# Feed-forward up projections: one 512-column product for the weight's high part, first group partly in the D banks, down projection two groups behind

## The chip, the cores and the metric

One core of a Trainium2 chip. The metric is the device time of one launch in microseconds, as the median of several runs. TensorE multiplies; VectorE, ScalarE and GpSimd (POOL) work on what it needs and leaves; loads from HBM are issued by SP's queue. Each engine works through its own instructions in program order.

## The reference, cut to what matters

A 4-layer encoder over 256 tokens of width 1024. Each layer is a SwiGLU feed-forward (FFN) half-step, a token mixer (attention, convolution, Fourier or gated linear attention) and a second FFN half-step, so there are eight FFN stages:

```python
def _swiglu(h, w1, w3, w2):
    return (jax.nn.silu(h @ w1) * (h @ w3)) @ w2

def reference(x, ...):
    h = x
    for i in range(DEPTH):                       # DEPTH = 4
        h = h + 0.5 * _swiglu(_rmsnorm(h, norm_g[i, 0]), ffn_w1[i, 0], ffn_w3[i, 0], ffn_w2[i, 0])
        u = _rmsnorm(h, norm_g[i, 1])
        ...                                      # mix = one of four mixers of u
        h = h + mix
        h = h + 0.5 * _swiglu(_rmsnorm(h, norm_g[i, 2]), ffn_w1[i, 1], ffn_w3[i, 1], ffn_w2[i, 1])
    return _rmsnorm(h, final_norm_g)
```

## The kernel before, in words

All is kept transposed: features on the 128 partitions, 256 tokens along the free axis. Weights and activations are float32. To multiply them in TensorE's fp32r form without losing bits, every operand is split into a high part (the value rounded to fp32r) and a low part (the rest), and a product is the sum of three: high times high, low of the one times high of the other, and the other way round (`mm3`, with the single product in line 69). The moving operand has 256 columns.

Weights come in blocks of 128x2048 (1 MB), in the order in which `plan` lists them. A load (`dma_block`, line 141, issued by SP) fills one of four `raw` buffers; `split_block` makes the high part `wh` on ScalarE (line 151) and the low part `wl` on VectorE (line 154), or on GpSimd where it is told so, into one of four pairs of buffers, and issues the next load. `done` counts blocks that TensorE has used up, and `pump(n)` splits as many new ones, at the place in the program where it is called.

An FFN stage (`ffn`) has 11 groups (NG) of 256 hidden features. `up(i, ...)` computes one 128x512 product per matrix: 8 steps k over the input features, 2 halves c of 128 hidden features, 3 products each, 48 in all, into one PSUM bank of the tag `ab`, of which there are four, used in turn. In the texts A0 is w1's product of group 0, B0 is w3's, and so on. `evac_a` multiplies A by the row factor R on VectorE (line 441) and applies silu on ScalarE (line 442); `evac_b` multiplies B by R (447), multiplies both (448) and splits the result into `gh` (ScalarE, 517) and `gl` (VectorE, 518). `down_add` adds w2's 48 products of a group into the four banks D0 to D3, which are held through the stage.

R is the normalization factor 1/rms of the tokens, spread over the partitions. x isn't multiplied by it before the up projection; the evacuations are. So `stats(True)` computes R while the first group's products run: two products with ones, then `newton_rsqrt` on VectorE, two integer operations and three steps of three operations (lines 348 to 356). In stages behind the first one it splits two weight blocks between, one of them on GpSimd.

The order of TensorE in a stage: A0 and B0 (k by k in turn, with `stats` behind k = 4, in the first stage behind k = 7), A1, B1, down of group 0, A2, B2, down of group 1, and so on. `DOWN_AFTER` says behind which group which down projection runs; groups 9 and 10 go into `down_final`, which finishes D0 to D3 one after the other, while `close_pair` adds them to h and makes the next stage's x. VectorE's and ScalarE's order is that of the program: at group 1 first the split and the evacuation of A0 and B0, then `evac_a` of A1, then two splits (`pump`), then B1's products and `evac_b(1)`. All is in program order on each engine (a manual schedule).

Of the kernel before, what the change touches and what calls it, by code (L numbers as in the profile page):

```python
# [21 lines left out]
DOWN_AFTER = {i: i - 1 for i in range(1, NG - 2)}  # L22
DOWN_AFTER[NG - 1] = NG - 3
NR = 4
NW = 4
# [15 lines left out]
class Enc:  # L41
# [31 lines left out]

    def mm3(self, out, l, r, start, stop, passes=(0, 1, 2)):
        (lh, ll), (rh, rl) = l, r
        for p in passes:
            self.mm(out, (lh, lh, ll)[p], (rh, rl, rh)[p], start and p == 0, stop and p == 2)
# [65 lines left out]
    def split_block(self, between=None, eng=None):  # L143
        b = self.nsplit
        if b >= len(self.blocks):
            return
        self.nsplit += 1
        raw = self.raw.pop(b)
        wh = self.sb(self.wp, [128, 2048], F32R, "wh", NW)
        wl = self.sb(self.wp, [128, 2048], F32R, "wl", NW)  # L150
        self.nc.scalar.activation(wh, raw, AF.Copy)  # L151
        if between:
            between()
        (eng or self.nc.vector).tensor_tensor(wl, raw, f32(wh), ALU.subtract)  # L154
        self.wsp[b] = (wh, wl)
        self.dma_block()

    def take(self, key):
        b = self.ntake
        self.ntake += 1  # L160
        assert self.blocks[b][0] == key, (self.blocks[b][0], key)
        wh, wl = self.wsp.pop(b)
        r = lambda t: t.rearrange("p (a b) -> p a b", a=self.blocks[b][1])
        return r(wh), r(wl)
# [17 lines left out]
    def setup(self):  # L182
# [9 lines left out]
        for b in first:  # L192
            self.raw[b] = self.sb(self.wp, [128, 2048], F32, "raw", NR)
            self.wsp[b] = (self.sb(self.wp, [128, 2048], F32R, "wh", NW), self.sb(self.wp, [128, 2048], F32R, "wl", NW))
# [19 lines left out]
        for j in range(4):  # L214
            self.normed(j)
            s = slice(512 * j, 512 * j + 512)
            for b in first:
                wh, wl = self.wsp[b]
                self.split(self.raw[b][:, s], wh[:, s], wl[:, s])
# [53 lines left out]
    def normed(self, j, h=None):  # L273
# [3 lines left out]
        if self.nstage < len(self.stages):  # L277
            xh = self.sb(self.hp, [128, 2, 256], F32R, f"xh{j}")
            xl = self.sb(self.hp, [128, 2, 256], F32R, f"xl{j}")
# [5 lines left out]
            self.xn[j] = (xh, xl)  # L285
        else:

            y = f32(self.sb(self.hp, [128, 2, 256], F32R, f"xh{j}"))
# [5 lines left out]
    def square(self, j, h=None, before_split=None):  # L294
# [17 lines left out]
        if j == 3:  # L312
# [5 lines left out]
            if self.row_norm():  # L318
                self.nsq = [self.sb(self.hp, [128, 256], F32R, "R", 2) for _ in range(2)]
                self.split(self.acc[:, 0], *self.nsq)  # L320
# [16 lines left out]
    def xk(self, k, t=None):  # L337
        xh, xl = self.x[k // 2]
        if t is None:
            return xh[:, k % 2, :], xl[:, k % 2, :]  # L340
        return xh[:, k % 2, 128 * t:128 * t + 128], xl[:, k % 2, 128 * t:128 * t + 128]

    def newton_rsqrt(self, y, r, shape, tag, bufs=2, pool=False):
# [6 lines left out]
        if pool:  # L350
            self.pump(1)
            self.pump(1, eng=nc.gpsimd)
        for n in range(3):
            nc.vector.tensor_tensor(t, r, r, ALU.mult)  # L354
            nc.vector.scalar_tensor_tensor(u, t, -0.5, y, ALU.mult, ALU.mult)  # L355
            nc.vector.scalar_tensor_tensor(r, u, 1.5, r, ALU.add, ALU.mult)  # L356

# [23 lines left out]
    def stats(self, row=False, scale=1.0):  # L381

        if row:
# [6 lines left out]
            self.newton_rsqrt(y, self.R, [128, 256], "nR", 1, self.nstage > 0)  # L390
            return
# [25 lines left out]
    def ffn(self, l, s):  # L417
# [6 lines left out]
        def up(i, names, hook={}):  # L424

            ws = [self.take((n, i)) for n in names]
            ps = [self.ab() for _ in names]
            for k in range(8):
                for w, p in zip(ws, ps):
                    for c in range(2):  # L430
                        sl = slice(128 * c, 128 * c + 128)
                        self.mm3(p[:, 256 * c:256 * c + 256], (w[0][:, k, sl], w[1][:, k, sl]), self.xk(k),
                                 start=k == 0 and c == 0, stop=k == 7)
# [5 lines left out]
        def evac_a(A):  # L439
            sl = self.sb(self.ev, [128, 2, 256], F32, "sl", 2)  # L440
            nc.vector.tensor_tensor(sl, self.v2(A), self.Rb(), ALU.mult)  # L441
# [3 lines left out]
        def evac_b(i, sl, B):  # L445
            br = self.sb(self.ev, [128, 2, 256], F32, "br", 2)
            nc.vector.tensor_tensor(br, self.v2(B), self.Rb(), ALU.mult)  # L447
            nc.vector.tensor_tensor(br, sl, br, ALU.mult)  # L448
            gh = self.sb(self.ev, [128, 2, 256], F32R, "gh", 3)
            gl = self.sb(self.ev, [128, 2, 256], F32R, "gl", 3)  # L450
            self.split(br, gh, gl)
            g[i] = (gh, gl)

        self.down_begin()
        first = self.nstage == 0
        A0, B0 = up(0, ("w1", "w3"), {7 if first else 4: lambda: self.stats(True)})
        for i in range(1, NG):
            A, = up(i, ("w1",))
            if i == 1:
                s0 = []  # L460
                self.pump(1, between=lambda: s0.append(evac_a(A0)), eng=nc.gpsimd if first else None)
                evac_b(0, s0[0] if s0 else evac_a(A0), B0)
            sl = evac_a(A)
# [24 lines left out]
    def dmm(self, w, g, d, k, stop=False, passes=(0, 1, 2)):  # L488
        if self.D4 is None:
# [4 lines left out]
                 (w[0][:, k, 128 * d:128 * d + 128], w[1][:, k, 128 * d:128 * d + 128]),  # L494
                 (g[0][:, k], g[1][:, k]), start=self.dfirst[j], stop=stop, passes=passes)
# [20 lines left out]
    def split(self, src, hi, lo):  # L516
        self.nc.scalar.activation(hi, src, AF.Copy)  # L517
        self.nc.vector.tensor_tensor(lo, src, f32(hi), ALU.subtract)  # L518
# [38 lines left out]
    def mix1(self):  # L557
# [13 lines left out]
        def pw1(i, names=("pa", "pg"), hook={}):  # L571
            ws = [self.take((n, i)) for n in names]
            ps = [self.ab() for _ in names]
            for k in range(8):
                for w, p in zip(ws, ps):
                    for c in range(2):
                        sl = slice(128 * c, 128 * c + 128)
                        self.mm3(p[:, 256 * c:256 * c + 256], (w[0][:, k, sl], w[1][:, k, sl]), self.xk(k),
# [95 lines left out]
        A0, G0 = pw1(0, hook={4: lambda: self.stats(True)})  # L674
# [88 lines left out]
        nn = self.sb(ev, [128, 4, 2, 256], F32R, "zs", 3)  # L763
        for i in range(4):
            if i < 2:
                hi, lo = (self.sb(self.hp, [128, 2, 256], F32R, f"x{t}{i}") for t in "hl")
            else:
                hi, lo = nn[:, 2 * i - 4], nn[:, 2 * i - 3]
# [9 lines left out]
            if i:  # L778
                for c in range(2):
                    self.split(zc[i][:, c], hi[:, c], lo[:, c])  # L780
            g.append((hi, lo))
# [21 lines left out]
    def mix2(self):  # L803
# [10 lines left out]
        def s1(g, banks):  # L814
            for t in range(2):
                for kk in range(2):
                    self.mm3(banks[t][:, 0:260], self.xk(2 * g + kk, t), tuple(half(w, kk) for w in cs),
                             start=kk == 0, stop=kk == 1)
            return banks

        def e1(g, banks):
            for t in range(2):
                h = self.sb(self.ev, [128, 260], F32R, f"a{g}{t}h")
                l = self.sb(self.ev, [128, 260], F32R, f"a{g}{t}l")
# [3 lines left out]
                ab[g][t] = (h, l)  # L828

        def s2(j):  # L830
# [3 lines left out]
            for c in range(2):  # L834
                for t in range(2):
                    for q in range(2):
# [3 lines left out]
                        h, l = ab[j][t]  # L840
                        self.mm3(p[:, 256 * c:256 * c + 256], (h[:, o:o + 128], l[:, o:o + 128]),
                                 (cs[0][:, t, r], cs[1][:, t, r]), start=n == 0, stop=t == 1 and q == 1)
                        n += 1
            gh = self.sb(self.ev, [128, 2, 256], F32R, f"m{j}h")
            gl = self.sb(self.ev, [128, 2, 256], F32R, f"m{j}l")
            self.split(self.v2(p), gh, gl)
            return gh, gl
# [29 lines left out]
    def mix0(self):  # L877
# [8 lines left out]
        def vproj(g, hf, hook=None):  # L886
            w = self.take(("v", g, hf))
            p = self.ab()
            for k in range(8):
                for t in range(2):  # L890
                    self.mm3(p[:, 256 * t:256 * t + 256], self.xk(k, t), (w[0][:, k, :], w[1][:, k, :]),
# [25 lines left out]
        def proj(hp, g):  # L917

            def step(k, state={}):
# [4 lines left out]
                for c in range(2):  # L924
                    sl = slice(128 * c, 128 * c + 128)
                    self.mm3(p[:, 256 * c:256 * c + 256], (w[0][:, k, sl], w[1][:, k, sl]), self.xk(k),
# [63 lines left out]
        def V(hp):  # L990
# [12 lines left out]
            if c == 0:  # L1003
                og[j] = (self.sb(ev, [128, 2, 256], F32R, f"og{j}h"), self.sb(ev, [128, 2, 256], F32R, f"og{j}l"))
            self.split(p[:, 0:256], og[j][0][:, c], og[j][1][:, c])
# [41 lines left out]
    def pre3(self):  # L1047
# [11 lines left out]
        wah, wal = self.sb(P, [128, 8, 64], F32R, "wah"), self.sb(P, [128, 8, 64], F32R, "wal")  # L1059
        self.split(wa, wah, wal)  # L1060
# [14 lines left out]
        return wah, wal, wa2, tri, lst, mask  # L1075

    def mix3(self):
# [15 lines left out]
        wah, wal, wa2, tri, lst, mask = self.pre  # L1093
# [6 lines left out]
        def qkproj(i, hook=None):  # L1100
            w = self.take(("gqk", i))
            p = self.ab()
            for k in range(8):
                for c in range(2):
                    sl = slice(128 * c, 128 * c + 128)
                    self.mm3(p[:, 256 * c:256 * c + 256], (w[0][:, k, sl], w[1][:, k, sl]), self.xk(k),
# [18 lines left out]
        for k in range(8):  # L1125
            self.mm3(pa[0:64, 0:256], (wah[:, k], wal[:, k]), self.xk(k), start=k == 0, stop=k == 7)
# [29 lines left out]
        def gate_c(d, t):  # L1156
            h = self.sb(ev, [128, 512], F32R, f"la{d}{t}h")
            l = self.sb(ev, [128, 512], F32R, f"la{d}{t}l")
            self.split(za[d, t], h, l)
            la[d, t] = (h, l)  # L1160
# [10 lines left out]
        def vproj(i):  # L1171

            def step(k, s):
# [3 lines left out]
                for t in range(2):  # L1177
                    self.mm3(p[:, 256 * t:256 * t + 256], self.xk(k, t), (w[0][:, k, :], w[1][:, k, :]),
# [11 lines left out]
        def rproj(i):  # L1190
            def step(k, s):
# [3 lines left out]
                for t in range(2):  # L1195
                    self.mm3(p[:, 256 * t:256 * t + 256], self.xk(k, t), (w[0][:, k, :], w[1][:, k, :]),
# [12 lines left out]
        def kstate():  # L1209

            for t in range(2):
# [5 lines left out]
                for d in range(2):  # L1217
                    p = bank()
                    h, l = la[d, t]
# [7 lines left out]
        og = {}  # L1227

        def head(hd):
# [4 lines left out]
            def decay(d):  # L1234
                p = bank()
                for t in range(2):
                    h, l = la[d, t]
# [45 lines left out]
            def out():  # L1283
# [19 lines left out]
                pool, tg = (self.hp, "x%s%d") if hd >= 2 else (ev, "og%s%d")  # L1303
                gh = self.sb(pool, [128, 2, 256], F32R, tg % ("h", hd))
                gl = self.sb(pool, [128, 2, 256], F32R, tg % ("l", hd))
                og[hd] = (gh, gl, o)

            def trans():
                gh, gl, o = og[hd]
# [221 lines left out]
```

## Time and profile before

| | before |
|---|---|
| median of 3 runs | 2022.13 us (2021.82 to 2023.69) |
| profiled execution | 2023.73 us, its span 2022.0 us |
| TensorE products busy | 1962.7 us, 97% of the span, 16496 products |
| VectorE busy | 1281.7 us, 63% |
| ScalarE busy | 898.5 us, 44% |
| GpSimd busy | 122.6 us, 6% |
| granted TensorE clock, mean | 0.987 of full speed |
| DMA | 338.59 MB, 167 GB/s in the mean |

Products are pipelined: a row's duration (0.28 us for 256 columns) reaches past the start of the next one. What a product costs in a dense stretch is read from the step between two starts, or from a stretch of the chain divided by its count. The time between a wait's end and the modelled end of the product before it is what the profile calls idle. The granted clock has two levels here, full speed (1.0, 2.4 GHz) and half (0.5, 1.2 GHz); a value between is a mean over a stretch.

### The profile page before, as it was taken

What the parts mean: (1) busy time and instruction counts of PE and PEld (TensorE: products, weight loads), DVE (VectorE), ACT (ScalarE), POOL (GpSimd) and SP (SyncE); (2) the same over time, 40 slices, a digit from 0 to 9 for tenths busy, and PEclk for the clock granted to TensorE, in tenths of its full rate; (3) what the DMA queues carried; (4) which work ended last, traced back from release to release, by engine and by line L of the source; (5) the groups of instructions that cost most, each with busy time, mean ns of one, the idle gap of its engine ahead of it and who ended that gap; (6) DMA issues with size and microseconds to landing.
All of it is one profiled execution on the core that took longest, in us unless ns stands there. A gap on an engine that the chain in (4) does not pass through costs nothing.

```text
span 2022.0 us, 36938 instructions
## 1 busy us (share of the span) xinstructions
PE 1962.7 (97%) x16496; PEld 1925.5 (95%) x16496; DVE 1281.7 (63%) x1374; ACT 898.5 (44%) x936; POOL 122.6 (6%) x93
## 2 busy tenths in 40 slices
PE   7999999999999998699999999999999999999998
PEld 7999999999999997499999999999999999999998
DVE  6655567755675575786557655765576555767554
ACT  4433544533444343444334444544444435754433
POOL 2000000000060011410001000000010000001000
PEclk9999999999999999799999999999999999999999
DMA  6555533455455533045554554355545554334551
GB/s 227 214 187 188 188 136 126 167 189 187 146 211 189 187 141 133 4 165 210 185 188 162 194 187 146 127 207 188 188 146 214 188 181 165 126 125 168 189 187 42
DMA packets 48671, 338.59 MB, mean 167 GB/s; under 512 B 5568, under 2 KB 5744, under 8 KB 8192
## 3 DMA queue, kind: packets, MB, share of 16 engines
q1 hardware_dynamic: 47952, 335.11, 45.5%
q8 instruction: 129, 2.11, 0.4%
q0 software_dynamic: 560, 1.12, 0.2%
q14 instruction: 30, 0.25, 0.0%
HBM read 335.16 MB, written 1.05 MB: 166 GB/s over the span
## 4 chain that ended last, share of the span: by engine, by line
PE 86%; DVE 9%; ACT 2%; issue 1%; DMA 0%; SPq 0%; POOL 0%; DVEq 0%; ACTq 0%; POOLq 0%
PE ab L69 55%; PE D L69 31%; DVE wl L154 2%; DVE nRt L354 2%; DVE zc L647 1%; ACT wh L151 1%; DVE nRu L348 0%; DVE R L356 0%; DVE nRu L355 0%; DMA raw<-in_ffn_w_dram 0%; PE D L72 0%; DVE gl L518 0%; DVE br L448 0%; PE ab L72 0%; DVE R L518 0%
## 5 line engine op out<-in xcount | busy, mean ns | idle before, releaser
L154 DVE TENSOR_TENSOR wl<-raw,wh 128x2048 fp32r<-128x2048 f32 x304 | 694.3, 2294 | 414.2 <-ACT wh L151 413.9
L69 PE MATMUL ab<-xh,wh 128*128 128x256 f32 x3200 | 911.3, 285 | 8.6 <-ACT wh L517 7.4
L69 PE MATMUL ab<-xh,wl 128*128 128x256 f32 x3200 | 908.7, 284 | 3.1 <-DVE wl L154 3.1
L69 PE MATMUL ab<-xl,wh 128*128 128x256 f32 x3200 | 908.5, 284 | 0.0
L151 ACT ACTIVATE wh<-raw 128x2048 fp32r<-128x2048 f32 x315 | 595.1, 1904 | 109.1 <-issue 84.0
L69 PEld LDWEIGHTS ab<-xh,wh 128*128 128x128 f32 x3200 | 617.4, 193 | 14.3 <-ACT wh L517 7.4
L69 PEld LDWEIGHTS ab<-xh,wl 128*128 128x128 f32 x3200 | 617.2, 193 | 3.5 <-DVE wl L154 3.3
L69 PEld LDWEIGHTS ab<-xl,wh 128*128 128x128 f32 x3200 | 617.2, 193 | 0.0
L69 PE MATMUL D<-gh,wh 128*128 128x256 f32 x1408 | 396.9, 282 | 7.3 <-ACT gh L517 7.3
L69 PE MATMUL D<-gl,wh 128*128 128x256 f32 x1408 | 400.5, 284 | 2.4 <-DVE gl L518 2.4
L69 PE MATMUL D<-gh,wl 128*128 128x256 f32 x1408 | 398.9, 283 | 0.0
L69 PEld LDWEIGHTS D<-gh,wh 128*128 128x128 f32 x1408 | 268.9, 191 | 8.5 <-ACT gh L517 8.5
L69 PEld LDWEIGHTS D<-gl,wh 128*128 128x128 f32 x1408 | 265.2, 188 | 3.9 <-DVE gl L518 3.9
L69 PEld LDWEIGHTS D<-gh,wl 128*128 128x128 f32 x1408 | 265.8, 189 | 0.0
L442 ACT ACTIVATE sl<-sl 128x512 f32<-128x512 f32 x88 | 55.6, 632 | 348.6 <-DVE sl L441 348.6
L517 ACT ACTIVATE gh<-br 128x512 fp32r<-128x512 f32 x88 | 55.6, 632 | 338.0 <-DVE br L448 338.0
L154 POOL TENSOR_TENSOR wl<-raw,wh 128x2048 fp32r<-128x2048 f32 x11 | 57.6, 5240 | 1135.4 <-ACT wh L151 805.4
L441 DVE TENSOR_TENSOR sl<-ab,R 128x512 f32<-128x512 f32 x88 | 60.6, 689 | 76.5 <-PE ab L69 75.7
L518 DVE TENSOR_TENSOR gl<-br,gh 128x512 fp32r<-128x512 f32 x88 | 61.4, 697 | 61.5 <-ACT gh L517 61.5
L282 ACT ACTIVATE xh<-h,cols 128x256 fp32r<-128x256 f32 x88 | 39.9, 500 | 73.8 <-DVE h L261 61.8
L447 DVE TENSOR_TENSOR br<-ab,R 128x512 f32<-128x512 f32 x88 | 60.6, 689 | 13.4 <-PE ab L69 13.4
L448 DVE TENSOR_TENSOR br<-sl,br 128x512 f32<-128x512 f32 x88 | 61.4, 698 | 4.9 <-ACT sl L442 1.4
(451 smaller groups left out, 1536.1 us busy)
## 6 DMA issues: line engine op xcount, KB each, us to landing
raw<-in_ffn_w_dram SPq DMA_DIRECT2D x262, 1024.0 KB, 4.8
raw<-in_attn_w_qk_dram SPq DMA_DIRECT2D x12, 1024.0 KB, 4.8
raw<-in_conv_w_pw_dram SPq DMA_DIRECT2D x12, 1024.0 KB, 4.8
raw<-in_gla_w_in_dram SPq DMA_DIRECT2D x12, 1024.0 KB, 4.8
raw<-in_attn_w_v_dram SPq DMA_DIRECT2D x6, 1024.0 KB, 4.8
raw<-in_fnet_w_dram SPq DMA_DIRECT2D x4, 1024.0 KB, 4.7
raw<-in_gla_w_o_dram SPq DMA_DIRECT2D x4, 1024.0 KB, 4.8
raw<-in_ffn_w_dram SPq DMA_DIRECT2D x8, 256.0 KB, 6.8
```

Of the source, the lines that this page charges most:

```text
L69: return self.nc.tensor.matmul(out, lhsT, rhs, start=start, stop=stop, skip_group_check=True)
L151: self.nc.scalar.activation(wh, raw, AF.Copy)
L154: (eng or self.nc.vector).tensor_tensor(wl, raw, f32(wh), ALU.subtract)
L282: nc.scalar.activation(xh[:, c], h[:, c], AF.Copy, scale=g[c])
L354: nc.vector.tensor_tensor(t, r, r, ALU.mult)
L441: nc.vector.tensor_tensor(sl, self.v2(A), self.Rb(), ALU.mult)
L442: nc.scalar.activation(sl, sl, AF.Silu)
L447: nc.vector.tensor_tensor(br, self.v2(B), self.Rb(), ALU.mult)
L448: nc.vector.tensor_tensor(br, sl, br, ALU.mult)
L517: self.nc.scalar.activation(hi, src, AF.Copy)
L518: self.nc.vector.tensor_tensor(lo, src, f32(hi), ALU.subtract)
L647: nc.vector.scalar_tensor_tensor(o, x, w, o, ALU.mult, ALU.add)
```

## The change

In `ffn`, and nowhere else in the arithmetic: for each k and half c, w's low part times x's high part is one product of 256 columns, and w's high part times both parts of x, which now lie side by side in one tile, is one of 512 columns. They fill a bank: the left half sums low times high and high times high, the right half high times low. So a product of a group takes two banks, one for each half c, and `both` brings the halves together: a ScalarE copy of the right half and a VectorE add of the left, for each bank. A's two banks come from `ab`, also B's, but for group 0, where B0 takes D1 and D2. R is multiplied behind that, into A's tile ahead of silu, and once more behind silu. The down projection of group i runs behind group i + 2. The Newton steps come back as a list: `factor` runs the short operations and one split behind k = 4; the first step follows A0's `both`, then a split, then the other two steps. No split in the FFN or conv stage's factor runs on GpSimd any more. All other edits rename the two parts of an operand into one tile of pairs; in the conv stage `factor` has two splits about the three steps.

```diff
-DOWN_AFTER = {i: i - 1 for i in range(1, NG - 2)}
-DOWN_AFTER[NG - 1] = NG - 3
+DOWN_AFTER = {i: i - 2 for i in range(2, NG)}
...
+    def pair(self, pool, shape, tag, bufs=1):
+
+        return self.sb(pool, [shape[0], 2, *shape[1:]], F32R, tag, bufs)
+
     def mm3(self, out, l, r, start, stop, passes=(0, 1, 2)):
-        (lh, ll), (rh, rl) = l, r
+
         for p in passes:
-            self.mm(out, (lh, lh, ll)[p], (rh, rl, rh)[p], start and p == 0, stop and p == 2)
+            self.mm(out, l[:, (0, 0, 1)[p]], r[:, (0, 1, 0)[p]], start and p == 0, stop and p == 2)
...
+    def newton_rsqrt(self, y, r, shape, tag, bufs=2, later=0):
 
         nc = self.nc
         t = self.sb(self.ev, shape, F32, tag + "t", bufs)
         u = self.sb(self.ev, shape, F32, tag + "u", bufs)
         nc.vector.tensor_scalar(u.bitcast(I32), y.bitcast(I32), 1, None, ALU.logical_shift_right)
         nc.vector.tensor_scalar(r.bitcast(I32), u.bitcast(I32), -1, 0x5F3759DF, ALU.mult, ALU.add)
-        if pool:
-            self.pump(1)
-            self.pump(1, eng=nc.gpsimd)
-        for n in range(3):
+
+        def step():
             nc.vector.tensor_tensor(t, r, r, ALU.mult)
             nc.vector.scalar_tensor_tensor(u, t, -0.5, y, ALU.mult, ALU.mult)
             nc.vector.scalar_tensor_tensor(r, u, 1.5, r, ALU.add, ALU.mult)
+
+        for _ in range(3 - later):
+            step()
+        return [step] * later
 
...
-            self.newton_rsqrt(y, self.R, [128, 256], "nR", 1, self.nstage > 0)
-            return
+            return self.newton_rsqrt(y, self.R, [128, 256], "nR", 1, 3)
...
         def up(i, names, hook={}):
 
+
             ws = [self.take((n, i)) for n in names]
-            ps = [self.ab() for _ in names]
+            ps = [[self.dbank(c + 1) if n else self.ab() for c in range(2)] for n in range(len(names))]
             for k in range(8):
+                x = self.xk(k)
                 for w, p in zip(ws, ps):
                     for c in range(2):
                         sl = slice(128 * c, 128 * c + 128)
-                        self.mm3(p[:, 256 * c:256 * c + 256], (w[0][:, k, sl], w[1][:, k, sl]), self.xk(k),
-                                 start=k == 0 and c == 0, stop=k == 7)
+                        self.mm(p[c][:, 0:256], w[:, 1, k, sl], x[:, 0], k == 0, False)
+                        self.mm(p[c].rearrange("p (q n) -> p q n", q=2), w[:, 0, k, sl], x, False, k == 7)
                 if k in hook:
                     hook[k]()
             self.done(len(names))
             return ps
 
-        def evac_a(A):
-            sl = self.sb(self.ev, [128, 2, 256], F32, "sl", 2)
-            nc.vector.tensor_tensor(sl, self.v2(A), self.Rb(), ALU.mult)
+        def both(ps, tag):
+
+            t = self.sb(self.ev, [128, 2, 256], F32, tag, 2)
+            for c in range(2):
+                nc.scalar.activation(t[:, c], ps[c][:, 256:512], AF.Copy)
+            for c in range(2):
+                nc.vector.tensor_tensor(t[:, c], t[:, c], ps[c][:, 0:256], ALU.add)
+            return t
+
+        def act_a(sl):
+            nc.vector.tensor_tensor(sl, sl, self.Rb(), ALU.mult)
             nc.scalar.activation(sl, sl, AF.Silu)
             return sl
 
         def evac_b(i, sl, B):
-            br = self.sb(self.ev, [128, 2, 256], F32, "br", 2)
-            nc.vector.tensor_tensor(br, self.v2(B), self.Rb(), ALU.mult)
+            nc.vector.tensor_tensor(sl, sl, self.Rb(), ALU.mult)
+            br = both(B, "br")
             nc.vector.tensor_tensor(br, sl, br, ALU.mult)
-            gh = self.sb(self.ev, [128, 2, 256], F32R, "gh", 3)
-            gl = self.sb(self.ev, [128, 2, 256], F32R, "gl", 3)
-            self.split(br, gh, gl)
-            g[i] = (gh, gl)
+            g[i] = self.pair(self.ev, [128, 2, 256], "g", 3)
+            self.split(br, g[i])
 
         self.down_begin()
-        first = self.nstage == 0
-        A0, B0 = up(0, ("w1", "w3"), {7 if first else 4: lambda: self.stats(True)})
+        steps = []
+
+        def factor():
+            steps.extend(self.stats(True))
+            self.pump(1)
+
+        A0, B0 = up(0, ("w1", "w3"), {4 if self.nstage else 7: factor})
+
+        sl0 = both(A0, "sl")
+        steps.pop(0)()
+        self.pump(1)
+        for f in steps:
+            f()
         for i in range(1, NG):
             A, = up(i, ("w1",))
+            sl = both(A, "sl")
             if i == 1:
-                s0 = []
-                self.pump(1, between=lambda: s0.append(evac_a(A0)), eng=nc.gpsimd if first else None)
-                evac_b(0, s0[0] if s0 else evac_a(A0), B0)
-            sl = evac_a(A)
+                self.pump(1)
+                evac_b(0, act_a(sl0), B0)
+            act_a(sl)
             self.pump()
...
+        def factor():
+            steps = self.stats(True)
+            self.pump(1)
+            for f in steps:
+                f()
+            self.pump(1)
+
+        A0, G0 = pw1(0, hook={4: factor})
         self.pump()
```

## Rows read from the trace of the kernel before

**Rows 1.** The page: busy time of the engines; the chain's shares by engine.

```profile
PE 1962.7 (97%) x16496; PEld 1925.5 (95%) x16496; DVE 1281.7 (63%) x1374; ACT 898.5 (44%) x936; POOL 122.6 (6%) x93
...
PE 86%; DVE 9%; ACT 2%; issue 1%; DMA 0%; SPq 0%; POOL 0%; DVEq 0%; ACTq 0%; POOLq 0%
```

**Rows 2.** The chain in order of time (start us, us, what), one group.

```profile
595.62 11.52 PE ab L69 x96
607.13 5.76 PE D L69 x48
```

**Rows 3.** Timeline of TensorE (start us, us): 512-column products, then 256-column ones.

```profile
1730.45 0.39 PE L69 MATMUL ab<-la00l,lst 128*128 128x512 f32 x1
1730.68 0.40 PE L69 MATMUL D<-la10h,lst 128*128 128x512 f32 x1
1730.92 0.40 PE L69 MATMUL D<-la10l,lst 128*128 128x512 f32 x1
1731.15 0.60 PE L72 MATMUL ab<-ident,kT 128*128 128x128 f32 x4
...
1731.82 0.40 PE L69 MATMUL D<-la01l,lst 128*128 128x512 f32 x1
...
1732.53 0.28 PE L69 MATMUL D<-tri,la00h 128*128 128x256 f32 x1
...
1732.88 0.28 PE L69 MATMUL D<-tri,la01l 128*128 128x256 f32 x1
```

**Rows 4.** Timeline of TensorE where a stage's second group ends; idle time in brackets.

```profile
568.37 0.28 PE L69 MATMUL ab<-xh,wl 128*128 128x256 f32 x1
570.02 0.39 PE L69 MATMUL D<-gh,wh 128*128 128x256 f32 x1 [1.36 <-ACT gh L517]
...
571.28 0.42 PE L69 MATMUL D<-gh,wl 128*128 128x256 f32 x1
...
571.92 0.41 PE L69 MATMUL D<-gh,wl 128*128 128x256 f32 x1
```

**Rows 5.** Who TensorE waited for: us in total, times, longest us.

```profile
PE D L69 <- ACT gh L517: 7.3, 6, 1.8
...
PE ab L69 <- DVE wl L154: 3.1, 1, 3.1
PE D L69 <- DVE gl L518: 2.4, 7, 0.5
```

**Rows 6.** Busy time by stretch, PEclk the mean granted clock; pauses, then a whole group.

```profile
571.40:578.20 6.80, 6.80 (x48) 6.80 (x47) 4.30 (x3) 4.23 (x3) 6.80 (x7) 0.78 0.21 65
...
1315.90:1329.90 14.00, 14.00 (x95) 14.00 (x96) 10.32 (x16) 6.22 (x6) 0.00 (x0) 0.78 0.51 193
595.50:612.80 17.30, 17.30 (x146) 17.30 (x146) 11.51 (x9) 8.78 (x7) 0.00 (x0) 1.00 0.62 237
```

**Rows 7.** Timeline of VectorE in the stage that starts at 545.2.

```profile
552.85 0.42 DVE L389 TENSOR_SCALAR R<-D 128x256 f32<-128x256 f32 x1
...
554.17 2.29 DVE L154 TENSOR_TENSOR wl<-raw,wh 128x2048 fp32r<-128x2048 f32 x1 [0.16 <-ACT wh L151]
556.38 4.85 DVE L354 TENSOR_TENSOR nRt<-R 128x256 f32<-128x256 f32 x1
...
564.48 0.43 DVE L356 SCALAR_TENSOR_TENSOR R<-nRu,R 128x256 f32<-128x256 f32 x1
565.01 0.69 DVE L441 TENSOR_TENSOR sl<-ab,R 128x512 f32<-128x512 f32 x1
...
573.99 5.02 DVE L154 TENSOR_TENSOR wl<-raw,wh 128x2048 fp32r<-128x2048 f32 x2 [2.50 <-ACT wh L151]
578.93 0.68 DVE L447 TENSOR_TENSOR br<-ab,R 128x512 f32<-128x512 f32 x1
```

**Rows 8.** A ScalarE copy out of PSUM: ns min/median/max, first and last start us.

```profile
L408 ACT ACTIVATE R<-D x2: 386/393/400, 226.5 to 1704.9; 128x256 f32<-128x256 f32 x2
```

**Rows 9.** A VectorE operation of 128x256 out of PSUM.

```profile
L389 DVE TENSOR_SCALAR R<-D x9: 418/425/425, 28.5 to 1826.6; 128x256 f32<-128x256 f32 x9
```

**Rows 10.** Timeline of GpSimd in that stage: its split.

```profile
556.02 4.93 POOL L154 TENSOR_TENSOR wl<-raw,wh 128x2048 fp32r<-128x2048 f32 x1 [5.94 <-ACT wh L151]
```

## What I expect, and from which rows

> **What bounds the kernel now.** I read the page first: TensorE carries 86% of the chain that ended last, VectorE 9% [rows 1]. The chain in order of time shows what the TensorE share is made of: inside a feed-forward stage it is an even beat, 96 up products in 11.52 us, then 48 down products in 5.76 us, with nothing between [rows 2]. That is 120.0 ns a product of 256 columns. Eight stages of 11 such groups of 17.28 us are 1,521 of the 2,022 us. In a whole group the other engines have room: VectorE is busy 11.5 of 17.3 us, ScalarE 8.8 [rows 6]. So two things are worth money: the price of a product, and what interrupts the beat. The list of waits names the interruptions in the feed-forward stages: 7.3 us for gh, 2.4 us for gl, 3.1 us for wl [rows 5]. They lie at one place of a stage, behind its first two groups of up products. Take the stage that starts at 545.2 (B1's last product starts at 568.37; it and the 193 before it at 120 ns lead back there): TensorE then stands until 570.02 for gh, and goes on in steps of about 215 ns [rows 4], because the granted clock has fallen (0.78 on average over the next 6.8 us [rows 6]). What it waits for is one line of work on VectorE, in program order: the factor R, the evacuation of A0 and B0, and weight splits of 2.3 us among them [rows 7].
>
> **The change, part by part.**
>
> *The wide product.* In each of 8 x 11 x 2 x 2 x 8 = 2,816 places (stage, group, matrix, half, k) three products of 256 columns become one of 256 and one of 512. Before: 360 ns. The trace has the new form: high and low parts times lst in 512 columns. Three steps of the first run, 1730.45 to 1731.15, take 233 ns each, three of the second, 1731.82 to 1732.53, 237; the 256-column products right behind them step by 117 [rows 3]. So the time goes with the columns; there is hardly a fixed part to save. I take 119 + 235 = 354 ns, 6 ns less, 16.9 us in all. Bounds: 2 x 120 = 240 ns for the wide one in the up products' own beat (no gain), and 106.7 ns of columns at 2.4 GHz plus the 13.3 ns that the 120 holds beside them, so 226.7 ns, 37 us gained. I take the value next to the 235 rows.
>
> The Trainium skill, page "TensorE: Matmul & The Clock Gate", section "Back-to-back issue gap", states a gap of N/2.4 + 2.5 ns, 216 ns at 512 columns. The rows do not agree (235, and 120 at 256). If the wide product reached 216 beside an unchanged 120, the part would be an estimated 68 us; that is a rival below.
>
> *The evacuation.* A product now fills two banks (x high and low side by side in each). It takes two ScalarE copies and two VectorE adds of 128x256 more; nearest rows 0.39 us [rows 8] and 0.43 us [rows 9], 0.44 taken with the issue. Per group VectorE takes on 4 x 0.43 = 1.7 us and ScalarE 1.6: 13.2 and 10.4 of 17 us, under TensorE's beat, which hides it; without that cover it would be 3.3 us a group.
>
> *The banks.* Four ab banks held four products; now they hold two. A0 takes ab 0 and 1, B0 takes D1 and D2, A1 ab 2 and 3, B1 ab 0 and 1, A2 ab 2 and 3, **B2 ab 0 and 1**, so B2 may start only when B1 has been evacuated. In the steady beat B1's successor comes 11 us later: nothing. At the start of a stage it decides, because of the next part. D1 and D2 have been read by the close of the stage before, whose last 2.9 us of products lie behind; nothing taken, 0.5 us a stage if VectorE lags.
>
> *The down projection one group later.* It takes 5.76 us of products out from between B1 and A2. TensorE then runs A0, B0, A1, B1, A2, B2 without a pause and wants w3 of group 2 and B1's banks 5.7 us earlier than the present order would. VectorE's list for it is no shorter. With S the start of the stage: the factor's three short operations and the split of w1 of group 1 end at 11.2, as now (552.85 and 554.17 [rows 7], S = 545.2). Two adds for A0 to 12.6, a Newton step of three operations to 14.0, the split of w3 to 16.3, two steps to 19.0, adds for A1 to 19.9. The split of w1 of group 2 runs 20.3 to 22.6: ScalarE's part stands behind A1's copies (A1 ends at 17.2). Then evac of A0, B0 and act of A1, which ping-pong between the two engines (multiply, silu, multiply, two adds, multiply, gh, gl, multiply, at 0.65 to 0.9 each): 28.3. silu 29.0, ScalarE's half of the split of w3 30.9, then **two** VectorE splits, w3 of group 2 and w2 of group 0, as pump() issues both before evac_b(1): 35.5 (the pair is the 5.02 us row at 573.99, and B1's first operation stands behind it at 578.93 today, too [rows 7]). One multiply and the first add: 36.6. TensorE is through with A2 at 28.7. **So it waits 7.9 us at B2**, with all of its queue behind it (B2, then the first down products). With every gap on VectorE closed the same work (23.6 us from 7.6 on) would end at 31.2: 2.5 us, the floor. In the first stage the factor comes behind its first group, and two splits are already done; the same list gives 5.4 us. Seven times 7.9 and 5.4: 60.7 us.
>
> After such a pause the clock is low for a while: 1.0 us lost over 48 products (6.80 for 5.76) after the shorter pause, 2.6 over 95 (14.0 for 11.4) after the 3.1 us one [rows 6]. I take 1.8 a stage, 14.4 us.
>
> *What goes.* The present waits for gh, gl and wl, 12.8 us, with 0.16 us for each of 14 because the wait is counted from the product's modelled end, 2.2; and their low clock, 2.6 + 1.0 + about 1.0 in the other stage of that form. Together 20 us. The GpSimd split goes with it: while it runs (556.02 to 560.95 [rows 10]) VectorE's first Newton operation takes 4.85 us, where the next of its kind take 0.43 [rows 7]. That is already in the forward list above (R ends at 19.0 instead of 564.91 - 545.2 = 19.7; the split that moves to VectorE eats the gain). On POOL what stands behind that split (the conv stage's preparation) starts earlier, and nobody waits for it. Raw loads on SP are released by the split that reads them, four ahead; the ones that a split now on VectorE releases arrive before they are wanted. Renamed pairs, the order lo before hi, and the conv stage's two splits: nothing, 1 us either way.
>
> Sum: 60.7 + 14.4 - 20 - 16.9 = +38 us. The profiled run took 2023.7 (span 2022.0 and 1.7 around it), 1.6 over the median, so 2,060 as a median.
>
> **Rivals.**
> 1. *The wide product streams at nearly one column a cycle* (512 in 216 ns). Then 24 ns go in each place, 68 us, the pause grows by some 0.7 us a stage, and the sum is about -7 (60.7 + 5.6 + 14.4 - 20 - 68): 2,015 us, faster. For it: the skill's gap rule above. Against it: six steps of 233 to 237 ns in the same data form. It decides the sign from about 20 ns saved a place on.
> 2. *The pause at B2 is near its floor*: ScalarE runs ahead so far that VectorE has no gaps. 8 x 2.5 + 10 of clock - 20 - 16.9 gives -7: 2,015 us, faster. For it: ScalarE has the time. Against it: the trace shows the same ping-pong today (VectorE idles 2.50 us before the pair of splits at 573.99, for ScalarE's part [rows 7]). It turns the sign at a pause of about 3.5 us a stage.
> 3. *The wide product saves nothing* (240 ns, the beat of 120 per 256 columns holds): the change then only pays the pause, 59 + 14.4 - 20: 2,076 us.
>
> **How the numbers follow.** Forecast 2,060, chance 0.62, its own range 2,040 to 2,078 (pause 7 to 9 us, clock 1.0 to 2.6, 2 to 13 ns saved a place). Rival 1: 0.12. Rival 2: 0.14. Rival 3: 0.12. Faster by over 0.2% (4 us, about what a measurement of this kernel can tell from no change): most of rivals 1 and 2, 0.23; within: 0.05; slower: 0.72. The range takes in rivals 1 and 2 about their middle and rival 3: 2,012 to 2,080.
>
> **What will show it.** A wait of TensorE of 7 to 9 us before a w3 product of the third group in each stage, released by VectorE's add, with a low granted clock behind it; steps of 119 and 235 ns in the up products; a steady group of about 17.1 us; no wait at the first down products; VectorE's first Newton operation at 0.43 us. It would be wrong if the steps were 216, or if evac_b(1) ran ahead of its splits.

## The result and the profile after

The changed kernel takes 2042.93 us as the median of 4 runs (2040.49 to 2043.78), the kernel before beside it 2022.47 us (2021.82 to 2023.69, 4 runs). The ratio is 1.0098, with a 95% interval of 1.0081 to 1.0116: 20 us slower. The profiled execution of after took 2040.49 us, its span is 2038.7 us against 2022.0, and the mean granted clock 0.976 against 0.987.

The page of after, its engines (the same view as [rows 1]):

```profile
PE 1939.5 (95%) x13680; PEld 1777.0 (87%) x13680; DVE 1385.3 (68%) x1735; ACT 1016.8 (50%) x1288; POOL 70.7 (3%) x84
```

TensorE has 2,816 products fewer and is busy for 23 us less, yet the span has grown by 17: what it gained, and more, it now spends standing. The list of waits of TensorE says where (the same view as [rows 5]; columns: who waits for whom, us in total, times, the longest):

```profile
PE ab L68 <- DVE br L446: 53.8, 8, 8.9
PE D L68 <- DVE R L320: 4.3, 1, 4.3
PE D L68 <- DVE h L260: 1.4, 1, 1.4
PE ab L68 <- DVE w L156: 1.4, 1, 1.4
```

The waits for gh and gl are gone. In their place stands one wait, once in each of the eight stages, for `br`: the sum of B's two halves. The chain of after in order of time through the stage that starts at 1074.82 shows who is late (start us, us, engine and what):

```profile
1086.32 5.21 PE ab L68 x30
...
1092.29 1.81 ACT w L153
1094.10 0.02 issue
1094.12 2.29 DVE w L156
1096.41 0.61 DVE sl L450
...
1097.05 0.64 ACT sl L451
...
1102.36 1.91 ACT w L153
1104.26 0.02 issue
1104.29 0.04 DVE w L156
1104.32 2.17 issue
1106.49 2.29 DVE w L156
1108.78 0.60 DVE sl L455
1109.38 0.34 DVE br L446
1109.72 0.04 issue
1109.77 7.92 PE ab L68 x32
1117.69 5.76 PE D L68 x48
1123.45 11.10 PE ab L68 x64
```

From 1091 on the chain leaves TensorE and runs through VectorE and ScalarE by turns until B1's first half has been added, 1109.72. Only then may B2 start: it uses the banks in which B1 lies. Two things more stand in the last three lines. B2's 32 products take 7.92 us (0.16 of it the modelled end of the last), where 64 in the next group take 11.10, so 5.55 for 32: the clock is low for them, 0.78 in the mean over the stretch from 1109.77 to 1120 that is shown below. And a group of 64 up products and 48 down products lasts 16.86 us, against 17.28 before [rows 2].

TensorE's own timeline at the stage's start and about the pause (compare [rows 4]), and two windows of after: a steady group, and the stretch behind the pause (compare [rows 6]; columns of the windows: us, busy time of PE, PEld, DVE, ACT and POOL, granted clock, DMA share, GB/s):

```profile
1074.82 0.86 PE L68 MATMUL ab<-x,w 128*128 128x256 f32 x4
...
1101.76 1.20 PE L68 MATMUL ab<-x,w 128*128 128x256 f32 x6
1109.77 2.50 PE L68 MATMUL ab<-x,w 128*128 128x256 f32 x7 [6.81 <-DVE br L446]
```

```profile
600.42:617.28 16.86, 16.86 (x114) 15.46 (x114) 11.49 (x12) 9.82 (x11) 0.00 (x0) 1.00 0.60 225
1109.77:1120.00 10.23, 10.23 (x53) 9.19 (x54) 5.86 (x8) 5.95 (x8) 0.00 (x0) 0.78 0.64 241
```

VectorE's timeline in the same stage (compare [rows 7]):

```profile
1083.19 2.28 DVE L156 TENSOR_TENSOR w<-raw,w 128x2048 fp32r<-128x2048 f32 x1
...
1086.46 0.42 DVE L350 TENSOR_TENSOR nRt<-R 128x256 f32<-128x256 f32 x1
...
1104.29 4.50 DVE L156 TENSOR_TENSOR w<-raw,w 128x2048 fp32r<-128x2048 f32 x2 [2.50 <-ACT w L153]
...
1109.30 0.74 DVE L446 TENSOR_TENSOR br<-br,ab 128x256 f32<-128x256 f32 x2
```

The first Newton operation takes 0.42 us, not 4.85; no GpSimd split runs beside it now. The pair of splits of 4.50 us, with 2.50 us of waiting for ScalarE's part in front of it, stands between A1's evacuation and B1's, as the prediction had placed it.

### The profile page after: what moved, and what is told of

Read it like the earlier page. It is cut to its first block, busy times and chain, and to the rows that moved or that the text cites. A ratio compares the mean times of both kernels' runs of the same rounds, so it can differ in the third digit from the quotient of the medians.

```text
span 2038.7 us, 31966 instructions
## 1 busy us (share of the span) xinstructions
PE 1939.5 (95%) x13680; PEld 1777.0 (87%) x13680; DVE 1385.3 (68%) x1735; ACT 1016.8 (50%) x1288; POOL 70.7 (3%) x84
## 4 chain that ended last, share of the span: by engine, by line
PE 86%; DVE 7%; ACT 4%; issue 2%; DMA 0%; SPq 0%; POOL 0%; DVEq 0%; ACTq 0%; POOLq 0%
PE ab L68 53%; PE D L68 32%; DVE w L156 3%; ACT w L153 2%; DVE zc L664 1%; DVE sl L450 1%; DVE sl L455 1%; DVE br L446 0%; DMA h<-in_x_dram 0%; PE D L71 0%; DVE br L457 0%; ACT sl L444 0%; ACT sl L451 0%; ACT g L534 0%; PE ab L71 0%
## 5 line engine op out<-in xcount | busy, mean ns | idle before, releaser
L68 PE MATMUL ab<-x,w 128*128 128x256 f32 (+1 forms) x6528 | 1124.6, 331 | 63.7 <-DVE br L446 53.8
L68 PEld LDWEIGHTS ab<-x,w 128*128 128x128 f32 x6528 | 980.5, 192 | 187.3 <-DVE br L446 56.4
L156 DVE TENSOR_TENSOR w<-raw,w 128x2048 fp32r<-128x2048 f32 x313 | 714.1, 2293 | 360.3 <-ACT w L153 358.0
L153 ACT ACTIVATE w<-raw 128x2048 fp32r<-128x2048 f32 x315 | 595.7, 1904 | 38.5 <-ACT w L153 21.8
L68 PEld LDWEIGHTS D<-g,w 128*128 128x128 f32 x4224 | 516.2, 188 | 3.0
L68 PE MATMUL D<-g,w 128*128 128x256 f32 x4224 | 518.5, 282 | 0.0
L446 DVE TENSOR_TENSOR sl<-sl,ab 128x256 f32<-128x256 f32 x176 | 66.7, 418 | 61.6 <-ACT sl L444 61.5
L68 PE MATMUL D<-x,w 128*128 128x256 f32 x448 | 82.6, 325 | 2.9 <-DVE h L260 1.4
L68 PEld LDWEIGHTS D<-x,w 128*128 128x128 f32 x448 | 69.6, 199 | 10.0 <-DVE h L260 2.4
L455 DVE TENSOR_TENSOR sl<-sl,R 128x512 f32<-128x512 f32 x88 | 60.5, 688 | 5.6 <-ACT sl L451 5.6
L450 DVE TENSOR_TENSOR sl<-sl,R 128x512 f32<-128x512 f32 x88 | 61.6, 700 | 2.5
```

Source lines behind the costliest of these rows:

```text
L68: return self.nc.tensor.matmul(out, lhsT, rhs, start=start, stop=stop, skip_group_check=True)
L153: self.nc.scalar.activation(w[:, 0], raw, AF.Copy)
L156: (eng or self.nc.vector).tensor_tensor(w[:, 1], raw, f32(w[:, 0]), ALU.subtract)
L446: nc.vector.tensor_tensor(t[:, c], t[:, c], ps[c][:, 0:256], ALU.add)
L450: nc.vector.tensor_tensor(sl, sl, self.Rb(), ALU.mult)
L455: nc.vector.tensor_tensor(sl, sl, self.Rb(), ALU.mult)
```

## The experiments

Three questions were asked: what the wide product is worth by itself, whether the pause comes from the banks, from the order of VectorE's work or from the delay of the down projection, and whether the change pays once the pause is small. Beside the experiments the kernel before ran again: 2022.53 us beside the product cut in two, the old delay in after, B1 in D0 and D3, and the early split; 2023.2 us beside the other three. The ratios below are to these.

### The wide product alone

The 512-column product is cut into two of 256 again, into the same banks, and all else stays as in after:

```diff
-                        self.mm(p[c].rearrange("p (q n) -> p q n", q=2), w[:, 0, k, sl], x, False, k == 7)
+                        for q in range(2):
+                            self.mm(p[c][:, 256 * q:256 * q + 256], w[:, 0, k, sl], x[:, q], False, k == 7)
```

> The changed kernel with the wide product taken apart again: high times x high and high times x low are two products of 256 columns into the same two banks; banks, evacuation, order and splits are the changed kernel's. It measures what the wide form alone is worth. By my prediction's price (354 ns instead of 360 a place) the time rises by 17 us to about 2060. By the changed kernel's trace (a group of 16.87 us where 17.28 were, so 347 ns a place) it rises by 37 us, less some 3 us because the pause at B2 shrinks when TensorE is slower: 2076. If the wide form saves nothing (rival 3) it stays at 2043. The wait before B2 stays at 6.5 to 7 us in all theories.

Measured: 2074.76 us, ratio to before 1.0258 (1.0243 to 1.0273), so 32 us more than after. The wait for B1's banks is the same to 1 us; the chain shows the old beat:

```profile
PE ab L68 <- DVE br L447: 54.7, 8, 8.8
```

```profile
609.23 11.52 PE ab L68 x96
620.74 5.76 PE D L68 x48
```

96 products in 11.52 us here, 64 in 11.10 us in after: 360.0 against 346.9 ns in each of the 32 places of a group, 13.1 ns saved. The change without its wide product would have cost 52 us; the wide product gives 32 of them back, about twice what the prediction gave it.

How the price of a product goes with its columns was then measured by making the other product of a place wide as well, which adds the low times low term to the sums:

```diff
-                        self.mm(p[c][:, 0:256], w[:, 1, k, sl], x[:, 0], k == 0, False)
+                        self.mm(p[c].rearrange("p (q n) -> p q n", q=2), w[:, 1, k, sl], x, k == 0, False)
```

> The changed kernel with the low part's product made wide, too (w's low part times both parts of x, so the low times low term is added): 2 products of 512 columns a place instead of one of 256 and one of 512. It measures the step of a wide product behind a wide one. If time goes with columns at the rate of the changed kernel's pair (346.6 ns for 768 columns, 0.45 a column): 231 ns each, 462 a place, 115 more, 325 us more in all, 2368. If the narrow product's 120 is a floor set by its weights and the wide one's true step is 226.7 (one column a cycle and 13.3): 453 a place, 300 us more, 2343. If 235 as in the kernel before: 470 a place, 347 us more, 2390.

Measured, in one run: 2303.04 us, span 2301.2. The chain of this kernel in a group that waits for nothing:

```profile
1203.11 0.91 PE ab L68 x4
1204.02 0.91 PE D L68 x4
1204.92 0.91 PE ab L68 x4
1205.83 0.91 PE D L68 x4
...
1216.07 7.27 PE ab L68 x32
```

12 products lie between 1203.11 and 1205.83: 226.7 ns each; 32 in 7.27 us are 227.2. A product of 256 columns takes 120.0. The difference, 106.7 ns, is 256 columns at 2.4 GHz, so both hold the same 13.3 ns beside their columns: 120.0 = 106.7 + 13.3, and 226.7 = 213.3 + 13.3. A place of after should then take 346.7, and it takes 346.9 by the chain. Three products of 256 columns pay the 13.3 ns three times, one of 256 and one of 512 twice. The total rose by 260 us instead of the 300 that the steps alone give, for the longer up products cover more of VectorE's work: the wait for br is 27.0 us here, and 53.8 in after, and the first stage's wait for R, 4.3 us in after, is gone. The remaining 9 us of the 40 were not traced.

### The pause: delay, banks or order

The delay of the down projection alone, in the kernel before:

```diff
-DOWN_AFTER = {i: i - 1 for i in range(1, NG - 2)}
-DOWN_AFTER[NG - 1] = NG - 3
+DOWN_AFTER = {i: i - 2 for i in range(2, NG)}
```

> The kernel before with one edit: the down projection runs two groups behind, as in the change. Products stay narrow, one bank each, so B2 takes the bank that B0 left, long free. Theory: the delay of the down projection costs nothing by itself; it costs because a product of the change takes two banks. Worked forward: the wait for gh and gl (1.9 us a stage) goes, a wait of about 1.5 us for the split of w3 of group 2 comes in its place; 0.4 us a stage less, 3 us in all, 2019. Rival (VectorE's list is too late for that order, whatever the banks): a wait of some 7 us a stage before B2 here, too, 40 us slower with the clock, 2062.

Measured: 2020.69 us, ratio 0.9991 (0.9982 to 1.0000). No wait for gh or gl is left, and the wait for a weight split, 3.1 us in one stage before, is now there in seven:

```profile
PE ab L68 <- DVE wl L153: 11.5, 7, 3.1
```

So the delay does what it looks like, it takes the down projection's waits away; but what they covered, the split of a weight, is late next and takes nearly the same. It costs nothing where a product needs one bank. The other way round, the old order comes back in after (the same three lines reversed):

> The changed kernel with the old order of the down projections (one group behind, none behind group 9). Bank theory: down of group 0 fills 5.8 us between B1 and A2, so B2 comes after its banks are free; TensorE instead waits for g of group 0, 4.3 us once a stage instead of 7.0; worked forward, 3.0 us a stage less, 24 us in all, 2019, a little under the kernel before. Rival (the pause is VectorE's list alone, and wherever the products stand they wait for its end): no change, 2043, the wait moves to the down product with the same 7 us.

Measured: 2016.89 us, ratio 0.9974 (0.9963 to 0.9984), 26 us less than after. The wait has moved back to the first down products, and is 30.0 us in sum where it was 53.8:

```profile
PE D L69 <- ACT g L535: 27.8, 8, 6.6
PE D L69 <- DVE g L536: 2.2, 7, 0.3
```

The delay costs 26 us in after, with its two-bank products and its other edits, and nothing in the kernel before, with one bank for a product: it takes both together. That it is the banks for which B2 waits in after, the next run shows. With the old order, 5.76 us of down products stand between B1 and A2, and TensorE wants B1's banks that much later.

The banks were tested by giving B1 others, D0 and D3, which the delayed down projection does not need until B2 is done:

```diff
-            ps = [[self.dbank(c + 1) if n else self.ab() for c in range(2)] for n in range(len(names))]
+            ps = [[self.dbank(c + 1) if n else self.dbank(3 * c) if (i, names) == (1, ("w3",)) else self.ab() for c in range(2)]
+                  for n in range(len(names))]
```

> The changed kernel with one edit: B1 goes into D0 and D3 (D0 is free once R's sum is read, D3 is not wanted before the first down projection), so B2 takes the banks of A0, free since the start of the stage. Bank theory: B2 then waits only for its own weights' split, 4.2 us instead of 7.0; 3.2 us a stage less, 26 us in all, 2017. Rival (B2 waits for its weights anyway, the banks come free in time): no change, 2043, wait before B2 7 us.

Measured: 2011.51 us, ratio 0.9942 (0.9926 to 0.9959), 31 us less than after. The wait for br has fallen from 53.8 to 1.1 us; the next late thing is the split of w3 of group 2, which B2 needs too:

```profile
PE ab L68 <- DVE w L156: 28.8, 8, 5.7
...
PE ab L68 <- DVE br L447: 1.1, 2, 0.7
```

So the bank is what B2 waits for in after. The first split of the pair, w3 of group 2, ends at 1106.49 in the chain of after, 3.2 us ahead of the bank at 1109.72 and 3.7 us behind the end of A2's products at 1102.8. With the bank out of the way B2 waits for that split, 28.8 / 8 = 3.6 us a stage.

The order on VectorE and ScalarE was tested with after's banks: the split of w3 of group 2 ahead of the evacuation of A0 and B0, and that of w2 of group 0 behind `evac_b(1)`:

```diff
-                self.pump(1)
+                self.pump(2)
...
-            self.pump()
+            if i > 1:
+                self.pump()
```

> The changed kernel with one edit in the order of VectorE and ScalarE at group 1: w3 of group 2 is split right behind w1 of group 2, ahead of the evacuation of A0 and B0, and w2 of group 0 behind evac_b(1) instead of ahead of it. The banks are as in the changed kernel. Bank theory: B1's evacuation no longer stands behind a pair of splits; B2 waits 3.4 us instead of 7.0, the releaser is still the add that empties B1's banks, 3.8 us a stage less, 30 us in all, 2013. Rival (the weights of B2 are the gate): the split of w3 is done 10 us earlier, so no wait at all is left before B2, 7 us a stage, 56 us in all, 1987.

Measured: 2009.67 us, ratio 0.9934 (0.992 to 0.9949), 33 us less than after:

```profile
PE ab L68 <- DVE br L446: 23.7, 8, 5.5
```

The pause is more than halved: most of it was the pair of splits in front of B1's evacuation, as the prediction had read from VectorE's order. What stays is the evacuation itself.

### Both remedies

B1 in D0 and D3, and w3 of group 2 split early, with w2 of group 0 left in its place:

```diff
-            ps = [[self.dbank(c + 1) if n else self.ab() for c in range(2)] for n in range(len(names))]
+            ps = [[self.dbank(c + 1) if n else self.dbank(3 * c) if (i, names) == (1, ("w3",)) else self.ab() for c in range(2)]
+                  for n in range(len(names))]
...
-                self.pump(1)
+                self.pump(2)
```

> The changed kernel with B1 in D0 and D3 and with w3 of group 2 split right behind w1 of group 2, ahead of the evacuation of A0 and B0 (w2 of group 0 keeps its place). Then neither B2's banks nor its weights are late. Theory: the wait before B2 is gone, a wait of about 2.2 us before the first down product (for the banks that hold B1 and for g) and one of about 1.2 us before B3 come; some 3.4 us a stage less than the changed kernel in waits and up to 2 more in clock where the shorter pause lets it stay up; 2005 to 2013. Rival (the list of VectorE is the limit, so what is taken at B2 comes back whole at the first down product): 2030 or more.

Measured: 1998.46 us (1996.63 to 2006.55, 5 runs), ratio 0.9886 (0.9868 to 0.9903). This beats both kernels, by 25 us and by 44 us. TensorE's timeline from B1 on, in the same stage as above:

```profile
1069.64 5.71 PE L68 MATMUL D<-x,w 128*128 128x256 f32 x32
1075.18 11.25 PE L68 MATMUL ab<-x,w 128*128 128x256 f32 x64
1087.71 6.02 PE L68 MATMUL D<-g,w 128*128 128x256 f32 x48 [1.27 <-DVE br L447]
1093.89 5.82 PE L68 MATMUL ab<-x,w 128*128 128x256 f32 x32 [0.17 <-DVE sl L447]
1100.68 5.92 PE L68 MATMUL ab<-x,w 128*128 128x256 f32 x32 [0.97 <-DVE br L447]
```

B1 (in D), A2 and B2 follow without a pause, and three short waits are left of one of 6.81 us. From the wait list of the whole kernel:

```profile
PE D L68 <- DVE br L447: 9.9, 7, 3.9
PE ab L68 <- DVE br L447: 8.2, 7, 2.8
```

The gain of 44 us is more than that of the waits (53.8 less 9.9 and 8.2 is 36). The rest goes with the clock: the products behind the short waits run at full clock here. 48 down products take 6.02 us with the modelled end of the last, 32 up products 5.82, where B2 took 7.92 in after; the mean granted clock is 0.988, in after 0.976. One stage is the exception, the one in which GpSimd prepares the convolution: 3.86 us of wait, then 48 down products in 8.29. The expectation was missed by 7 us on the fast side: it left 3.4 us of waits in a stage, and 2.3 are left (9.9 and 8.2 over eight).

## Why the prediction was right, and where it was off

The prediction was 2060 us with a range of 2012 to 2080, slower by chance 0.72. The time is 2043 us, inside that range and 17 us below the forecast. The sign and the mechanism were right; the term of the wide product was mis-sized by 20.6 us, more than the whole miss. The pause came out 5.6 us shorter than forecast, and smaller terms of the sum below, with the 4 us by which the medians lie further apart (20) than the profiled executions (17), make up the rest.

**The pause at B2: right.** Forecast 7.9 us in seven stages and 5.4 in the first. Start to start less one step, it is 7.0 us in the stage above, with 8.9 as the longest wait of the eight and 53.8 us the sum, or 55.1 with 0.16 of modelled end in each, against 60.7; the first stage has 4.6. The list that was worked out from VectorE's rows holds step by step, each end 0.5 to 1.6 us early, counted from the start of the stage: the factor's split ends at 10.7 (forecast 11.2), the Newton steps at 18.0 (19.0), the split of w1 of group 2 at 21.6 (22.6), the pair of splits at 34.0 (35.5), B2 starts at 35.0 (36.6). TensorE reaches B2 at 28.0, not 28.7, for A0 to A2 run at the cheaper place. What shortened the list is small and spread: 0.5 us each up to the factor's split, in the Newton steps and in the evacuations. The two moves that were tested on it, the banks and the order, each took off about half of the pause; for the banks that is what must come if the split ends late (by 3.7 us) and the bank later still (by 7.0). One thing of the list was priced at nothing and was not: GpSimd's preparation of the convolution, which starts at 557.95 instead of 568.78, now runs beside VectorE's Newton steps and splits, and that stage waits 8.95 us where the other six behind the first wait 6.6 to 6.8.

**The clock: right in kind, a little small.** 1.8 us a stage were taken, 14.4 in all. B2's 32 products take 7.34 to 8.55 us in the eight stages, 61.84 together, or 60.5 without 0.16 of modelled end in each, where eight times 5.55 are 44.4: 16.1 us.

**What goes: right.** The waits for gh and gl are gone, and their low clock with them. That clock was read a little low: by the chain of before the products behind the three pauses took 7.40, 7.16 and 14.20 us for 47, 47 and 94 of them, 5.7 us lost and not 4.6, so 20.7 us go and not 20. VectorE's first Newton operation takes 0.42 us. The first stage's wait for R fell from 6.3 to 4.3 us, which was not forecast.

**The evacuation: hidden, as forecast.** In the steady group of 16.86 us VectorE is busy 11.49 and ScalarE 9.82 (forecast 13.2 and 10.4).

**The wide product: the step that failed.** The prediction named both ends, 0 and 37 us, and took 16.9 "next to the 235 rows" [rows 3]. Measured are 13.1 ns a place by the groups and 13.3 by the steps, 36.9 to 37.5 us for 2,816 places, so the upper bound itself; in the comparison with the wide product cut in two it is 32 us of measured time. The bound had the right form: columns at 2.4 GHz and 13.3 ns beside them. What was wrong was to conclude from six steps, in a stage of another kind, that "the time goes with the columns; there is hardly a fixed part to save". The steady up products had shown 13.3 ns beside the columns, 120.0 against 106.7, in the rows ahead of those [rows 2], over 144 products. That these 13.3 ns belong to the product and not to its columns, rows of 256 columns alone could not tell; the run with two wide products a place shows it. Had the prediction taken 226.7, its sum would have come to 38 - 20.6 = +17 us, 2,040. The Trainium skill, page "TensorE: Matmul & The Clock Gate", section "Back-to-back issue gap", gives N/2.4 + 2.5 ns for the isolated gap; the trace agrees with its slope (106.7 ns for 256 columns more) and not with its fixed part, which is 13.3 ns in this kernel at both lengths.

**The sum over the profiled executions.** The waits for br 53.8, with 0.16 us of modelled end for each of eight 1.3; the two small new waits of 1.4 us 2.8; the clock 16.1; less 20.7 for what goes; less 37.5 for the wide product: +15.8 us. Other waits in the lists changed by -2.0 (R in the first stage), -1.5, -1.2, -0.9 and +1.1, so +11.3 us are accounted for. The span grew by 16.7. Part of the 5 us between is the clock of a mixer, 0.90 in the mean from 1705 to 1730 in after where the kernel before has 1.00 from 1685 to 1730; the rest was not traced.

**The new wait on D1 and D2**, taken at nothing, is there once, 1.4 us at one stage's start (the row for h in the wait list of after).

**The rivals.** A product at 216 ns: the dense stretches of the kernel with two wide products a place give 226.7; it would have needed about 20 ns saved a place to turn the sign, and 13.3 were saved. A pause near its floor of 2.5 us: not so in after, for VectorE idles 2.50 us ahead of the pair of splits, as it did before; with the order and banks changed it does get there (waits of 0.17 to 1.27 us in the last kernel), and the sign turns, as that rival said it would below about 3.5 us a stage. With the wide product worth more than it took, the sign turns at a longer pause than that: the kernel with B1 in D0 and D3 still waits 3.6 us a stage and is 11 us faster than before. No saving at all, 2,076 us: the cut-in-two kernel, which has exactly no saving, measured 2,075.

**What stays open.** Why the 512-column products of [rows 3] take 235 ns, 8 ns more than in a dense stretch, was not tried. The comparison of after with its wide product cut in two gives 32 us where the steps give 37.5. Between the two profiled executions it is 33.5 us, and the waits in the list of the kernel cut in two are 2.0 us shorter in sum; the rest was not traced.

## What to carry to other kernels

A wider product that saves its fixed part also takes twice the accumulator banks, so list which product next uses each bank and when the engine that empties it gets there in its own program order: the 37 us saved here were lost, nearly twice over, in eight pauses of which two placements (B1's banks, one split earlier) take most away. Moving work out from between two users of a buffer isn't free: that work was the cover under which the buffer was emptied. Take the price of a product from the longest dense run of the same stage, not from the few that have the right shape; and where it is to be split into columns and a fixed part, measure it at two lengths.

## What was not expected of the hardware

- A product of 128x128 fp32r weights and its own weight load costs its columns at 2.4 GHz and 13.3 ns: 120.0 ns for 256, 226.7 for 512 back to back, 346.9 for one of each by turns, all in dense stretches of the feed-forward stages.
- The price of a pause in clock does not follow its length. In the kernel with both remedies waits of 0.17 to 1.27 us cost next to none. But after the same wait before B2, 3.57 us in two stages of the kernel with B1 in D0 and D3, its 32 products take 8.38 or 7.39 us (5.71 at full clock, with the modelled end of the last); after 2.61 us in two stages of the kernel with the early split, 5.82 or 7.43. The first two lines are of the one, the others of the other. Why equal waits cost differently was not tested.

```profile
379.30 8.38 PE L68 MATMUL ab<-x,w 128*128 128x256 f32 x32 [3.57 <-DVE w L156]
1094.03 7.39 PE L68 MATMUL ab<-x,w 128*128 128x256 f32 x32 [3.57 <-DVE w L156]
381.75 5.82 PE L68 MATMUL ab<-x,w 128*128 128x256 f32 x32 [2.61 <-DVE br L446]
1090.20 7.43 PE L68 MATMUL ab<-x,w 128*128 128x256 f32 x32 [2.61 <-DVE br L446]
```

- VectorE is slower beside GpSimd's work in more than one place. In the stage at 560 us GpSimd prepares the convolution's taps from 557.95 to 579.8, and in that time VectorE's operations that take 0.42 us elsewhere take 0.6 to 0.8; that stage has the longest pause:

```profile
559.85 19.90 POOL L570 TENSOR_TENSOR wd<-m,wt 128x256 f32<-128x256 f32 x21
565.86 0.72 DVE L350 TENSOR_TENSOR nRt<-R 128x256 f32<-128x256 f32 x1
586.11 8.55 PE ab L68 x32
```
